# Cross attention's queries: seven block products per pair of heads in place of two plain projections, in a two-layer decoder trunk

## The chip, the cores and the metric

The kernel runs on one core of one Trainium2 chip. The metric is the device time of one launch in microseconds (us), the median of the runs. The engines are named as in the profile: PE (TensorE, matmuls), PEld (its weight loads), DVE (VectorE), ACT (ScalarE), POOL (GpSimd), SP (SyncE, which issues most loads). Each engine works through its own queue in order.

## The reference

A trunk of two layers over 512 tokens of width 1024, with 256 memory tokens. Each layer is a half-step SwiGLU FFN, a token mixer (layer 0: differential attention; layer 1: a pooling mixer), cross attention into the memory with 4 heads of 256, and a second FFN; each is followed by a LayerNorm of a scaled residual sum. The part that the change touches:

```python
def memory_cross_attention(x, mem, wq, wkv, wo):
    q = (x @ wq).reshape(B, S, XA_HEADS, XA_HEAD_DIM)          # wq 1024x1024
    k, v = jnp.split(mem @ wkv, 2, axis=-1)                    # wkv 1024x2048
    ...
    s = jnp.einsum('bshd,bmhd->bhsm', q, k) * (XA_HEAD_DIM ** -0.5)
    p = jax.nn.softmax(s, axis=-1)
    o = jnp.einsum('bhsm,bmhd->bshd', p, v).reshape(B, S, D_MODEL)
    return o @ wo

x = layer_norm(a * x + h, ...)                                 # h: the mixer
x = layer_norm(a * x + memory_cross_attention(x, mem, ...), ...)
```

## The kernel before, in words

**Products.** Every product is in fp32 split into two parts: a "high" part `wh` or `xh`, rounded by a copy on ACT, and a "low" part `wl` or `xl`, the difference, by a subtraction on DVE (`split`, lines 114 and 115; `split_scaled`, 119 and 120, for scaled queries). One product step is three matmuls, high by high, low input, low weight (`mm3`, lines 201, 202 and 203). A weight piece is 128x1024 of fp32, 512 KB: it is loaded into a raw tile, copied to a high and subtracted to a low tile.

**Cross attention** has, for each of four heads, keys and values of the memory (`xa_kv`: 48 matmuls of 256 columns to PSUM tile `pk`, 48 to `pv`), queries (`project` into `xq`: two 128-wide column blocks x 8 steps x 3 = 48 matmuls of 512 columns), and the scores, softmax and weighted values (`xa_head`, PSUM `xs`, `pt`, `xo`). `xa_main` is the main line; `xa_side` gives the heads' side work, and `weave` puts a side step between the products when 2500 ns of estimated matmul time have passed. `to_tokens` ends the stage with the output product (`ps`) and the next LayerNorm. Of the two layers' queries there are 8 heads x 48 = 384 matmuls of 512 columns.

**Into the stage.** The mixer's last products add to the residual `X` (`ln_add`, line 397); `ln_token` then does a token block's LayerNorm: the mean (L406, DVE), squares on ACT, the reciprocal deviation on POOL, and two passes on DVE (L423, L425). `turn` transposes a normalized block of 128 tokens on PE into PSUM tiles `pt` (L479), and splits them into `xh`, `xl`, the stage's input, feature rows on the partitions. With two 512-feature halves that is two ACT copies and two DVE subtractions of 128x512 per token block. The blocks are called tokens 0 to 3. While the last LayerNorms run, PE is given keys and values: in layer 0 head 0's, in layer 1 heads 0 and 1's (`early_kv`), woven into the pooling mixer.

**Loads.** In layer 0 weights for queries, keys and values come 1 MB at a time through 2 raw tiles (`raw_cols`) on SP's queue, with 5 high and 5 low tiles. In layer 1 512 KB pieces go through two tags, `raw` (2) and `rawe` (3), split into `wh`/`wl` or `we`. Layer 0 also writes the split memory (`mem`) to DRAM, 4 x 512 KB (`keep_memory`, SP's queue), for layer 1 to load again.

**Seven products.** The FFNs already compute their 2x2-block products with seven block products instead of eight. The x block sums for that are called factors; `turn` stores a token's transposes as `self.factors` when the next stage is an FFN. The order of instructions on each engine comes from the program's order and a scheduler's priorities; `issue_after` puts an instruction behind another.

Of the kernel before, what the change touches and what calls it, by code (L numbers as in the profile page):

```python
# [96 lines left out]
WAIT = object()  # L97


def drain(units):  # L100
    for _ in units:
        pass


class Trunk:
# [57 lines left out]
    def stage_pools(self, w, raw, order):  # L163

        with ExitStack() as ctx:
# [8 lines left out]
            self.w_bufs, self.raw_bufs, self.aux_turn = w, raw, 0  # L174
            self.w_order, self.raw_order = [("wh", "wl")], ["raw"]
# [9 lines left out]
    def aux(self, name, tag=None):  # L185
        if tag is None:
            tag = list(self.banks)[self.aux_turn % 3]
            self.aux_turn += 1
# [66 lines left out]
    def load(self, shape, src, tag=None):  # L255
# [4 lines left out]
        self.nc.sync.dma_start(t, src)  # L260
        return t

    def load_cols(self, w, c0, tag=None):
        if "rawe" not in self.stage:
# [5 lines left out]
    def load_wide(self, w, c0, tag=None):  # L270
        if "rawe" not in self.stage:
# [50 lines left out]
    def rows(self, w, k0, kn, c0, homes=None):  # L322
# [3 lines left out]
        for k in range(0, kn, 4):  # L326
# [5 lines left out]
            if "rawe" in self.stage:  # L332
# [122 lines left out]
    def turn(self, t, half, two_pass=None):  # L455
# [6 lines left out]
        if self.ln_next == "ffn":  # L462
# [687 lines left out]
    def pool_mixer(self, layer, ln):  # L1150
# [35 lines left out]
        self.w_order = [("wh", "wl")] * 3 + [("we", "we")] * 2  # L1186
        self.raw_order = ["rawe"] * 3 + ["raw"] * 2
        self.begin_ln(layer, ln, 1.0)
        for t in range(NT):
# [17 lines left out]
            self.turn_late()  # L1207
# [41 lines left out]
    def xa_kv(self, w, h, ahead=None):  # L1249
        nc = self.nc  # L1250
        rk = ahead or self.load_cols(w, h * 256)
        ps = self.mm("pk").rearrange("p (c n) -> p c n", c=2)
        for j in range(2):
            wk = rk[j] if ahead else self.halves(rk[j])
            for k in range(KC):
# [3 lines left out]
        kv = lambda: tuple(  # L1259
            self.kvp.tile([P, 2, MEM], F32R, tag="kv", name="kv", bufs=8) for _ in range(2)  # L1260
        )
        kt = kv()
        self.turn_late()
        self.split(kt[0], kt[1], ps)
        wv = self.halves_wide(self.load_wide(w, D + h * 256))
        ps = self.mm("pv").rearrange("p (m n) -> p m n", m=2)
        for m in range(2):
            o = slice(m * P, (m + 1) * P)
            for k in range(KC):
                mt = self.memT[k]  # L1270
                yield self.mm3(ps[:, m], (mt[0][:, o], mt[1][:, o]), wv[k], k == 0, k == KC - 1)
        v = kv()
        self.split(v[0], v[1], ps)
        return kt, v

    def xa_head(self, qs, kt, v):
# [3 lines left out]
        for tt in range(0, NT, 2):  # L1280
            sc = self.aux("xs").rearrange("p (t n) -> p t n", t=2)
            for i in range(2):
                o = slice((tt + i) * P, (tt + i + 1) * P)
                for c in range(2):
                    q = qs[c]
                    self.mm3(
                        sc[:, i], (q[0][:, o], q[1][:, o]), (kt[0][:, c], kt[1][:, c]), c == 0, c == 1
                    )
# [12 lines left out]
        for tt in range(0, NT, 2):  # L1301
# [8 lines left out]
            yield  # L1310
# [209 lines left out]
```

## Time and profile before

| | us |
|---|---|
| median of 3 runs | 1952.09 |
| runs | 1949.88, 1952.63, 1952.09 |
| the profiled execution's own time | 1952.38 |
| its span | 1950.6 |
| PE busy | 1918.7 (98%) |
| DVE busy | 1560.5 (80%) |
| ACT busy | 1012.7 (52%) |
| POOL busy | 336.1 (17%) |

The span is from the first to the last instruction on record; the run's time is 1.8 us more. Cross attention of layer 0 starts at about 601 us of the span, with the first `pk` matmul, and that of layer 1 at about 1455. A row of a timeline gives the start, the duration, the engine, the line, what is written and read, the shape, and in square brackets an idle time before it with what released it. A matmul's duration overlaps its neighbours', so that its cost is the distance of two starts. A row `x2` has two instructions.

### The profile page before, as it was taken

The page shows a single profiled execution, that of the slowest core. Times are in us where ns is not written, and L with a number is a line of the kernel's source. Part 1 is how long each engine was busy: PE and PEld are TensorE (multiplying, and loading weights), DVE is VectorE, ACT ScalarE, POOL GpSimd, SP SyncE. Part 2 cuts the span into 40 slices and gives each one's busy share as a digit, 9 for nine tenths or more (in the row PEclk, how much of TensorE's full clock was granted, in tenths as well). Part 3 has the DMA queues.
Part 4 walks back from the last instruction along what each step waited for, and adds up shares of the span by engine and source line. Part 5 has one row for each costly group of instructions (what it writes and reads, how often), then busy time and mean ns, then how long its engine had stood idle before and what let it go on. Part 6 is the DMA issues. An engine that isn't in the chain of part 4 may idle for free.

```text
span 1950.6 us, 32439 instructions
## 1 busy us (share of the span) xinstructions
PE 1918.7 (98%) x13052; PEld 1746.2 (90%) x13052; DVE 1560.5 (80%) x2200; ACT 1012.7 (52%) x1537; POOL 336.1 (17%) x317
## 2 busy tenths in 40 slices
PE   9999999999999999999999999999999999999998
PEld 8999998888778888989998999999888889999996
DVE  7988987788867557798887888888876468888886
ACT  6555553466655444555554555455445436555552
POOL 3212121111211002312210322112110013111211
PEclk9999999999999999999999999999999999999999
DMA  9888772322135325977695598778435336778861
GB/s 253 197 174 180 167 152 66 90 65 87 44 108 177 126 65 141 218 171 147 149 200 143 105 210 173 174 162 163 153 119 162 109 87 116 189 172 172 182 143 44
DMA packets 254182, 280.58 MB, mean 144 GB/s; under 512 B 9168, under 2 KB 221648, under 8 KB 254032
## 3 DMA queue, kind: packets, MB, share of 16 engines
q0 software_dynamic: 95808, 102.77, 32.4%
q1 hardware_dynamic: 158224, 175.74, 28.3%
q8 instruction: 102, 1.67, 0.3%
q14 instruction: 48, 0.39, 0.1%
HBM read 274.28 MB, written 4.20 MB: 143 GB/s over the span
## 4 chain that ended last, share of the span: by engine, by line
PE 79%; DVE 13%; ACT 3%; issue 3%; DMA 2%; POOL 1%; SPq 0%; DVEq 0%; POOLq 0%; ACTq 0%
PE x L201 7%; PE x L202 7%; PE x L203 7%; PE z L201 4%; PE z L202 4%; PE z L203 4%; PE ps L203 4%; PE ps L202 4%; PE ps L201 4%; DVE wl L115 3%; PE px L201 2%; PE px L203 2%; PE px L202 2%; PE y L203 2%; PE xq L201 2%
## 5 line engine op out<-in xcount | busy, mean ns | idle before, releaser
L636 POOL DMA_DIRECT2D ra<-in_ffn_w_in_dram x132 | 170.5, 1315 | 993.3 <-DVE wl L115 971.3
L114 ACT CAST wh<-ra 128x1024 fp32r<-128x1024 f32 x184 | 193.3, 1052 | 213.8 <-PE x L202 67.7
L115 DVE TENSOR_TENSOR wl<-ra,wh 128x1024 fp32r<-128x1024 f32 x184 | 223.6, 1220 | 70.8 <-ACT wh L114 64.7
L114 ACT CAST wh<-rc 128x1024 fp32r<-128x1024 f32 x136 | 142.9, 1053 | 120.6 <-PE x L202 45.5
L201 PE MATMUL x<-xh,wh 128*128 128x256 f32 x704 | 197.1, 280 | 1.5 <-ACT xh L114 0.8
L203 PE MATMUL x<-xh,wl 128*128 128x256 f32 x704 | 196.6, 279 | 1.9 <-DVE wl L115 1.9
L202 PE MATMUL x<-xl,wh 128*128 128x256 f32 x704 | 196.3, 279 | 0.0
L201 PE MATMUL x<-xe,wh 128*128 128x256 f32 x704 | 195.7, 278 | 0.0
L202 PE MATMUL x<-xe,wh 128*128 128x256 f32 x704 | 195.6, 278 | 0.0
L203 PE MATMUL x<-xe,wl 128*128 128x256 f32 x704 | 195.5, 278 | 0.0
L114 ACT CAST wh<-b 128x1024 fp32r<-128x1024 f32 x112 | 117.8, 1051 | 131.8 <-PE x L202 63.5
L115 DVE TENSOR_TENSOR wl<-rc,wh 128x1024 fp32r<-128x1024 f32 x136 | 164.4, 1219 | 22.9 <-ACT wh L114 22.9
L115 DVE TENSOR_TENSOR wl<-b,wh 128x1024 fp32r<-128x1024 f32 x112 | 136.7, 1221 | 41.6 <-ACT wh L114 41.6
L201 PEld LDWEIGHTS x<-xh,wh 128*128 128x128 f32 x704 | 133.0, 189 | 3.5 <-ACT xh L114 1.1
L203 PEld LDWEIGHTS x<-xh,wl 128*128 128x128 f32 x704 | 133.3, 189 | 2.4 <-DVE wl L115 2.4
L202 PEld LDWEIGHTS x<-xl,wh 128*128 128x128 f32 x704 | 133.4, 189 | 1.5 <-DVE xl L115 0.2
L201 PEld LDWEIGHTS x<-xe,wh 128*128 128x128 f32 x704 | 132.6, 188 | 1.4
L202 PEld LDWEIGHTS x<-xe,wh 128*128 128x128 f32 x704 | 132.5, 188 | 1.3
L203 PEld LDWEIGHTS x<-xe,wl 128*128 128x128 f32 x704 | 132.5, 188 | 0.0
L203 PE MATMUL y<-xh,wl 128*128 128x256 f32 x352 | 99.1, 281 | 2.1 <-DVE wl L115 1.2
L201 PE MATMUL y<-xh,wh 128*128 128x256 f32 x352 | 98.2, 279 | 0.1
L201 PE MATMUL z<-xe,wh 128*128 128x256 f32 x352 | 97.9, 278 | 0.0
(404 smaller groups left out, 6085.8 us busy)
## 6 DMA issues: line engine op xcount, KB each, us to landing
ra<-in_ffn_w_in_dram POOLq DMA_DIRECT2D x132, 512.0 KB, 6.9
rc<-in_ffn_w_in_dram SPq DMA_DIRECT2D x88, 512.0 KB, 6.2
b<-in_ffn_w_out_dram SPq DMA_DIRECT2D x60, 512.0 KB, 4.9
ra<-in_ffn_w_in_dram SPq DMA_DIRECT2D x44, 512.0 KB, 4.7
rc<-in_ffn_w_in_dram POOLq DMA_DIRECT2D x44, 512.0 KB, 7.5
b<-in_ffn_w_out_dram POOLq DMA_DIRECT2D x16, 512.0 KB, 13.0
raw<-in_da_w_qkv_dram SPq DMA_DIRECT2D x16, 512.0 KB, 5.1
raw<-in_xa_wkv_dram SPq DMA_DIRECT2D x8, 1024.0 KB, 5.4
```

The costliest lines, as they stand in the source:

```text
L114: self.nc.scalar.copy(hi, src),
L115: self.nc.vector.tensor_sub(lo, src, hi.bitcast(F32)),
L201: mm(out, w[0], x[0], start=start, stop=False, skip_group_check=again)
L202: mm(out, w[0], x[1], start=False, stop=False, skip_group_check=again)
L203: self.last_mm = mm(out, w[1], x[0], start=False, stop=stop, skip_group_check=again)
L636: self.last_more = nc.gpsimd.dma_start(t, source(*block), accum_op=ALU.add)
```

## The change

- **Queries.** `queries` handles a pair of heads (512 columns of `wq`) as a 2x2 block product: block rows are 512 features, block columns one head, input blocks 512 features by 256 tokens. Seven products of 24 matmuls with 256 columns replace 2 x 48 with 512, so a layer has 336 narrow for 192 wide ones. They run in the order factor 0 (weight r1), 1 (r2), 3 (r3), 6 (r4), 4, 5, 2.
- **Weight sums.** The third weight, r3, gets a second 512 KB added in its raw tile by an accumulating transfer on POOL's queue ahead of the first product; the other three sums are additions of 128x1024 on DVE (line 1408 after), in the raw tiles. So each of r1 to r4 stays in a raw tile from its load to its last use.
- **Input sums.** `x_factors` makes the factors for tokens 2 and 3 as they are transposed: two sums of 128x1024 of tokens 0 and 1, then per token an ACT copy, four sums and five splits. Tokens 0 and 1 are stored plainly.
- **Combining.** The products are combined by copies on ACT and additions of 128x512 on DVE, and four scaled splits per pair.
- **Order.** Keys and values yield in steps (`MARK`), interleaved with products. In layer 1 only head 0's keys and values are woven into the mixer, head 1's with the first pair's products. The weave's gap is 2200 instead of 2500.
- **Loads and tiles.** In layer 0 now 512 KB pieces through 5 raw tiles, with 4 high and 4 low tiles; in layer 1 2 high and 2 low tiles (3 and 3 before) beside 4 `we`.
- **Memory.** `keep_memory` is put behind the stage's last weight load on SP's queue (its four writes stand after the first four loads of the output weights).

The instructions: PE 13,095 rows against 12,809, DVE 1,990 against 1,900, ACT 1,157 against 1,103, POOL 190 against 185, SP 229 against 220.

```diff
@@ Trunk.turn
-        if self.ln_next == "ffn":
+        if self.ln_next in ("ffn", "xa"):
             hi, lo = self.factors[half]
@@ pool_mixer
-        self.w_order = [("wh", "wl")] * 3 + [("we", "we")] * 2
+        self.w_order = [("wh", "wl")] * 2 + [("we", "we")] * 2
...
-            self.turn_late()
+            if self.late and self.late[0] < 2:
+                self.turn_late()
             self.ln_token(t)
@@ x_factors (new)
+        temps = [self.tmp("q", (P, 4, H)) for _ in range(6)]
+        s3, a11, a12, a21, s1, s2 = temps
+        def part(i, x, o):
+            self.split(F[i][0][:, :, o], F[i][1][:, :, o], x)
+        for r, (hi, lo) in zip((a11, a12), F):
+            nc.vector.tensor_tensor(r, hi.bitcast(F32), lo.bitcast(F32), ALU.add)
+        yield
+        for t in (2, 3):
...
+            nc.scalar.copy(b21, pts[0])
+            nc.vector.tensor_tensor(t1, pts[1], b21, ALU.subtract)
+            part(3, t1, o)
+            part(2, pts[1], o)
+            nc.vector.scalar_tensor_tensor(t2, t1, -1.0, a11[:, :, o], ALU.mult, ALU.subtract)
+            nc.vector.scalar_tensor_tensor(t1, t2, -1.0, a12[:, :, o], ALU.mult, ALU.subtract)
+            part(6, t1, o)
+            yield
+            part(4, t2, o)
+            nc.vector.tensor_tensor(t3, a11[:, :, o], b21, ALU.subtract)
+            part(5, t3, o)
+            yield
@@ queries (new)
+        r1 = self.load([4, H], source(1, 1), tags[0])
+        r2 = self.load([4, H], source(2, 1), tags[1])
+        r3 = self.load([4, H], source(1, 2), tags[2])
+        nc.gpsimd.dma_start(r3, source(1, 1), accum_op=ALU.add)
+        yield MARK
+        x = bank(self.mm("xq"))
+        yield from product(x, r1, 0, True)
...
+        yield from product(y, r2, 1, True)
+        nc.vector.tensor_tensor(p1, y, p1, ALU.add)
+        qa = self.pair("q", (P, 2, S))
+        keep(qa, first, p1, 1)
+        yield MARK
+        r4 = self.load([4, H], source(2, 2), tags[3])
+        z = bank(self.aux("z", "yz"))
+        yield from product(z, r3, 3, True)
...
+        yield from product(z, r4, 6, then=(r4, r3))
+        yield MARK
+        yield from product(x, r4, 4, then=(r1, r4, ALU.subtract))
...
+        yield from product(x, r1, 5, then=(r2, r4))
...
+        yield from product(x, r2, 2)
@@ xa_main
-            for p in ((0, 2 * P), (2 * P, S)) if self.late else ((0, S),):
-                for c in range(2):
-                    yield from self.project(ps[c], ws[c], (p,))
-                    self.turn_late(1 - c)
...
+        ready = self.x_factors()
+        if not layer:
+            k = self.xa_kv(wkv, 0)
+            next(k)
+            yield from step(k)
+            self.turn_late(2)
+            yield from step(k)
+        self.late = []
+        next(ready)
+        if not layer:
+            for _ in range(2):
+                yield from step(k)
+                next(ready)
+        for u in range(XA_H // 2):
+            q = self.queries(wq, u, tags)
+            next(q)
+            k = self.xa_kv(wkv, u + 1, bank="yz")
+            next(k)
+            order = (k, q, k, q, k, q, k, q, q, q, q) if layer and not u else (q, k) * 4 + (q,) * 3
+            for g in order:
+                yield from step(g)
+                next(ready, None)
+        yield from whole(self.xa_kv(wkv, XA_H - 1))
@@ xa
-        self.weave(self.xa_main(layer), self.xa_side(), 2500)
+        self.weave(self.xa_main(layer), self.xa_side(), 2200)
...
-            self.keep_memory()
+            with self.tc.issue_after(self.last_load.ins):
+                self.keep_memory()
@@ pools
+    def xa_pools(self):
+        order = ("wh", "wl", "raw")
+        return self.stage_pools(dict(wh=4, wl=4), dict(raw=5), order, True)
...
-        return self.stage_pools(dict(wh=3, wl=3, we=4), dict(raw=2, rawe=3), order)
+        return self.stage_pools(dict(wh=2, wl=2, we=4), dict(raw=2, rawe=3), order, True)
@@ cross mixer of layer 1
-                    self.weave(self.early_kv(layer, (0,), ahead), side, 900, 6000)
-                drain(self.early_kv(layer, (1,)))
+                self.weave(whole(self.xa_kv(w, 0, ahead)), side, 900, 6000)
```

DVE's queue in layer 0, before, from the end of token 3's LayerNorm on (`X3`; `pt` are transposed tokens, `pk` keys, `raw` a raw weight):

```order
L425 SCALAR_TENSOR_TENSOR X3_79<-X3_79,rstd_6677,v_6459 128x1024
L115 TENSOR_TENSOR xl_6467<-pt_6851,xh_6465 128x4x128
L115 TENSOR_TENSOR xl_6468<-pt_6858,xh_6466 128x4x128
L115 TENSOR_TENSOR kv_6850<-pk_6792,kv_6849 128x512
L115 TENSOR_TENSOR xl_6467<-pt_6865,xh_6465 128x4x128
L115 TENSOR_TENSOR xl_6468<-pt_6872,xh_6466 128x4x128
L115 TENSOR_TENSOR wl_6947<-raw_6944,wh_6946 128x1024
L115 TENSOR_TENSOR wl_6951<-raw_6944,wh_6950 128x1024
```

The same place after the change (`q` are temporaries of the input sums):

```order
L441 SCALAR_TENSOR_TENSOR X3_79<-X3_79,rstd_6677,v_6459 128x1024
L130 TENSOR_TENSOR kt_6860<-pk_6800,kt_6859 128x512
L1370 TENSOR_TENSOR q_6864<-xh_6465,xl_6467 128x1024
L1370 TENSOR_TENSOR q_6865<-xh_6465,xl_6467 128x1024
L1384 TENSOR_TENSOR q_6867<-pt_6907,q_6866 128x4x128
```

Behind the LayerNorm the two wide sums now come first. Further on in the same queue, DVE after the change up to the split of head 1's second key weight (`xe` are factors 4 to 6, `y` and `p` the second product and its sum):

```order
L1392 TENSOR_TENSOR q_6863<-q_6864,q_6866 128x4x128
L130 TENSOR_TENSOR xe_6795<-q_6867,xe_6792 128x4x128
L1440 TENSOR_TENSOR p_6999<-y_7055,p_6999 128x512
L130 TENSOR_TENSOR xe_6794<-q_6863,xe_6791 128x4x128
L130 TENSOR_TENSOR wl_7090<-raw_6968,wh_7089 128x1024
```

Five rows stood before the first weight split; now 26 stand between the LayerNorm and `wl_7090`, five of them 128x1024.

DVE's queue in layer 1 after, from the second sum of tokens 0 and 1 to the split of factor 3 for token 3, the third product's input:

```order
L1370 TENSOR_TENSOR q_16296<-xh_16084,xl_16086 128x1024
L1384 TENSOR_TENSOR q_16298<-pt_16347,q_16297 128x4x128
L130 TENSOR_TENSOR kt_16429<-pk_16313,kt_16428 128x512
L1387 SCALAR_TENSOR_TENSOR q_16299<-q_16298,q_16295 128x4x128
L1392 TENSOR_TENSOR q_16294<-q_16295,q_16297 128x4x128
L130 TENSOR_TENSOR xl_16087<-q_16298,xh_16085 128x4x128
L130 TENSOR_TENSOR xl_16087<-pt_16347,xh_16085 128x4x128
L1388 SCALAR_TENSOR_TENSOR q_16298<-q_16299,q_16296 128x4x128
L1384 TENSOR_TENSOR q_16298<-pt_16437,q_16297 128x4x128
L1440 TENSOR_TENSOR p_16391<-y_16452,p_16391 128x512
L130 TENSOR_TENSOR xe_16293<-q_16298,xe_16290 128x4x128
L130 TENSOR_TENSOR xl_16087<-q_16298,xh_16085 128x4x128
```

Before, the tokens' plain splits stood here, one behind the other, between weight splits:

```order
L115 TENSOR_TENSOR wl_16211<-rawe_16206,wh_16210 128x1024
L115 TENSOR_TENSOR xl_15840<-pt_16107,xh_15838 128x4x128
L115 TENSOR_TENSOR xl_15841<-pt_16114,xh_15839 128x4x128
L115 TENSOR_TENSOR wl_16215<-rawe_16208,wh_16214 128x1024
L115 TENSOR_TENSOR kv_16185<-pv_16135,kv_16184 128x512
L115 TENSOR_TENSOR we_16282<-rawe_16276,we_16281 128x1024
```

Two rows of 128x512 per token block have become nine, and the weight splits stand behind them.

195 lines of the change are left out of this document (136 added, 59 removed).

## The prediction

> **What bounds the kernel now.** First the page's busy shares and its chain that ended last: they say whose time the span is.
>
> ```profile
> PE 1918.7 (98%) x13052; PEld 1746.2 (90%) x13052; DVE 1560.5 (80%) x2200; ACT 1012.7 (52%) x1537; POOL 336.1 (17%) x317
> PE 79%; DVE 13%; ACT 3%; issue 3%; DMA 2%; POOL 1%; SPq 0%; DVEq 0%; POOLq 0%; ACTq 0%
> ```
>
> TensorE (PE) is busy for 98% of the span, so fewer matmul columns are worth their time, wherever nothing else ends late. But VectorE (DVE) is 80% busy over the whole program and holds 13% of the chain: there is little slack to give it work. Then the busy times by window, in the two stretches of cross attention that the change rewrites (columns: window, then PE, PEld, DVE, ACT, POOL busy with their counts, the granted clock, the DMA share, GB/s).
>
> ```profile
> 615.20:745.00 129.80, 129.80 (x775) 113.89 (x775) 69.76 (x112) 52.63 (x101) 0.00 (x0) 1.00 0.34 109
> 1456.80:1460.20 3.40, 3.15 (x15) 3.15 (x16) 2.95 (x6) 2.55 (x5) 0.18 (x1) 0.50 0.03 9
> 1480.00:1500.00 20.00, 20.00 (x146) 18.84 (x146) 9.56 (x15) 10.04 (x17) 0.00 (x0) 1.00 0.60 172
> ```
>
> In layer 0 PE has no gap from 615.2 to 745.0 while DVE is busy for 69.8 of 129.8 us. In layer 1 the stretch from 1480 is full too, but ahead of it there is one of 3.4 us at half clock. PE's timeline shows what brought that: two idles of over a microsecond within 2 us.
>
> ```profile
> 1455.51 0.38 PE L201 MATMUL pk<-mem,wh 128*128 128x256 f32 x1 [1.24 <-ACT wh L241]
> 1457.05 1.12 PE L479 MATMUL pt<-ident,X 128*128 128x128 f32 x4 [1.04 <-DVE X L425]
> ```
>
> So in these stages a wait of PE is paid once as idle and can be paid again in clock: 3.4 us at half speed is 1.7 us of work.
>
> **The sum is made against the profiled execution**, 1952.38 us, 0.29 above the median of 1952.09.
>
> **Queries: 384 matmuls of 512 columns become 672 of 256.** Steady rows of each shape on PE's timeline of layer 1:
>
> ```profile
> 1474.45 0.39 PE L201 MATMUL xq<-xh,wh 128*128 128x512 f32 x1
> 1479.81 0.39 PE L203 MATMUL xq<-xh,wl 128*128 128x512 f32 x1
> ```
>
> These are 23 matmuls apart: 5.36 / 23 = 0.233 us each. The narrow shape stands in the keys of layer 0:
>
> ```profile
> 605.07 0.28 PE L202 MATMUL pk<-mem,wh 128*128 128x256 f32 x1
> 607.57 0.28 PE L203 MATMUL pk<-mem,wl 128*128 128x256 f32 x1
> 608.68 0.28 PE L203 MATMUL pv<-wh,mem 128*128 128x256 f32 x1
> 609.15 0.28 PE L201 MATMUL pv<-wh,mem 128*128 128x256 f32 x1
> ```
>
> The keys' two rows are 22 apart, 0.1136 each; the values' are 4 apart, 0.1175. I take 0.1155. Each layer loses 192 x 0.233 = 44.7 and gains 336 x 0.1155 = 38.8, which is -5.9; both layers **-11.8** (-13.1 at 0.1136, -10.4 at 0.1175). The Trainium skill, page "TensorE: Matmul & The Clock Gate", section "Back-to-back issue gap", gives a lone matmul's gap as N/2.4 + 2.5 ns, that is 215.8 and 109.2 ns, by which the saving would be only 9.5 us and the sum below +3.6. The rows above are longer for both widths, and they decide.
>
> **Layer 0: DVE gets a queue that PE catches up with.** The plain stores of tokens 2 and 3 were two DVE rows each; now two sums of 128x1024 come first, then nine rows of 128x512 per token. Rows of DVE that give the prices (a row's start to the next one's):
>
> ```profile
> 604.64 1.22 DVE L115 TENSOR_TENSOR wl<-raw,wh 128x1024 fp32r<-128x1024 f32 x1
> 605.77 1.28 DVE L423 SCALAR_TENSOR_TENSOR X<-X,mean,v 128x1024 f32<-128x1024 f32 x1
> 608.11 1.28 DVE L425 SCALAR_TENSOR_TENSOR X<-X,rstd,v 128x1024 f32<-128x1024 f32 x1
> 609.30 1.28 DVE L115 TENSOR_TENSOR xl<-pt,xh 128x512 fp32r<-128x512 f32 x2
> 610.50 0.68 DVE L115 TENSOR_TENSOR kv<-pk,kv 128x512 fp32r<-128x512 f32 x1
> 611.10 1.27 DVE L115 TENSOR_TENSOR xl<-pt,xh 128x512 fp32r<-128x512 f32 x2
> ```
>
> A 128x1024 row takes 1.13, one of 128x512 0.60. From 609.3, when the last token's LayerNorm leaves DVE, the new queue up to the low half of head 1's second key weight (the row wl_7090) holds 6 wide and 21 narrow rows: 6 x 1.13 + 21 x 0.60 = 19.4, so it is there at 628.7. PE, from the transposes at 607.68, has ahead of the first matmul that reads it 126 matmuls of 256 (14.6) and 16 transposes (1.6): it is there at 623.8. PE then idles **4.9 us**, if DVE never waits. But its rows follow ACT's copies, and one weight (head 1's first value piece) can only be issued when the fifth raw tile is free; with the waits that I find by walking both queues it is up to 7.0. I take 6.0. Behind the waiting matmul the whole of PE's queue stands, the third product among it. Two idles that add up to 2.3 us brought the half clock above, so +1.7 (0 to 1.7). Nothing later gives this back: from 615.2 to 745.0 PE had no idle that could shrink.
>
> **Layer 1: the same at the third product.** Rows of DVE there:
>
> ```profile
> 1463.22 0.68 DVE L397 SCALAR_TENSOR_TENSOR X<-X,ps 128x512 f32<-128x512 f32 x1
> 1463.82 1.22 DVE L243 TENSOR_TENSOR we<-rawe,we 128x1024 fp32r<-128x1024 f32 x1
> 1468.72 1.41 DVE L423 SCALAR_TENSOR_TENSOR X<-X,mean,pooled 128x512 f32<-128x512 f32 x2
> 1470.04 1.41 DVE L425 SCALAR_TENSOR_TENSOR X<-X,rstd,pooled 128x512 f32<-128x512 f32 x2
> 1471.37 0.68 DVE L115 TENSOR_TENSOR kv<-pk,kv 128x512 fp32r<-128x512 f32 x1
> ```
>
> From 1463.22, until the third product's input of token 3 is split, the new queue holds a LayerNorm sum (0.60), three weight splits (3.4), the mean (0.1), two passes of LayerNorm (1.32 each), the two wide sums (2.3) and 11 narrow rows (6.6): 15.6, so 1478.9, and up to 1480.7 where it waits for POOL and ACT. PE has in that time, after the transposes of token 2 (its row is below), 46 matmuls of 256 and token 3's transposes, then 49 matmuls to the third product.
>
> ```profile
> 1463.59 1.03 PE L479 MATMUL pt<-ident,X 128*128 128x128 f32 x8
> ```
>
> That is 1463.6 + 0.8 + 5.3 + 0.8 + 5.7 = 1476.2, an idle of 2.7 to 4.5; I take **3.6**, and +1.7 of clock (0 to 1.7). Against it stand before's own idles on this stretch, of which some go: -0.9 (-0.5 to -1.3, from the 1.24 and 1.04 above and this one):
>
> ```profile
> 1465.10 0.39 PE L203 MATMUL pk<-mem,we 128*128 128x256 f32 x1 [0.47 <-DVE we L243]
> ```
>
> **Weight sums and combinations.** A pair adds three 128x1024 sums, three adds of 128x512 and four scaled splits in place of the two per head: 3 x 1.13 + 3 x 0.60 = 5.2 us of DVE and about 1 us of ACT copies per pair, 10 us a layer. After the first third product PE's 130 us cover it (DVE is busy 70 of them), and PE is in front nowhere else by my walk but at the second pair's start: **+1.0** (0 to 2) for the two layers. If the cover were gone, 20 us of DVE would be on the path. The early sum is an accumulating transfer on POOL's queue, ahead of product 3 by two products (5.5 us) and the keys between. The nearest rows:
>
> ```profile
> ra<-in_ffn_w_in_dram POOLq DMA_DIRECT2D x132, 512.0 KB, 6.9
> raw<-in_da_w_qkv_dram SPq DMA_DIRECT2D x16, 512.0 KB, 5.1
> ```
>
> A plain 512 KB on POOL's queue lands in 6.9; even twice that is earlier than the split of r3 stands in DVE's queue (629 in layer 0, if issued by 612), so 0; a gain is excluded since before had no such wait. **The memory's write** (four transfers of 512 KB on SP's queue) moves from about 600 us behind the output weights' first four loads: both places are under a full PE, and in the second nothing that PE needs within 10 us is issued behind it: 0 on either side.
>
> The sum: -11.8 + 6.0 + 1.7 + 3.6 + 1.7 - 0.9 + 1.0 = **+1.3**, so 1953.7 for such an execution and, 0.3 lower, about **1953.5** for the median. All terms at their low ends: -13.1 + 4.9 + 0 + 2.7 + 0 - 1.3 + 0 = -6.8; at the high ends: -10.4 + 7.0 + 1.7 + 4.5 + 1.7 - 0.5 + 2.0 = +6.0.
>
> **Rivals.**
>
> *Faster: the queues keep pace and the clock holds.* DVE never waits for ACT, and the idles leave the clock alone: -11.8 + 4.9 + 2.7 - 1.3 = -5.5, or 1946.6 for the median. For it stands a stretch of layer 0's mixer with 1.34 us of PE idle and the clock at 1.00:
>
> ```profile
> 498.00:504.00 6.00, 4.66 (x28) 3.80 (x28) 5.22 (x13) 3.74 (x10) 1.16 (x1) 1.00 0.04 15
> ```
>
> Against it: the two idles here would be nearly three and over four times as long. Chance 0.25.
>
> *About the same, with one fall of the clock fewer.* The one idle of 3.6 us in layer 1 may leave the clock as that single one did, where it fell after two with work between them: 1.7 less, 1951.8. By the Trainium skill, page "TensorE: Matmul & The Clock Gate", Part 1, the clock goes down after an idle window of about 3.4 us; the fall at 1456.8, after idles of 1.24 and 1.04, doesn't agree with so long a window. Chance 0.12.
>
> *Slower: the raw tiles are the bound.* In layer 0 r1 to r3 hold three of the five raw tiles, and head 1's two key pieces, its two value pieces and r4 pass through the other two, each issued only when a split before it is done. r4 is issued when the row wl_7090 is done (628.7 or later) and, by the 5.1 above, lands at 634; copy and split make it 636, and PE reaches it at about 636.5. That has half a microsecond to spare. If such a load takes the 6.9 of POOL's queue, or the cast stands behind another copy, each of the four pairs waits 1 to 1.5 us more: +4 to +6 on the sum, about 1958.5. It decides from 5.6 us of landing upward. For it: the stretch from 1480 already moves 172 GB/s. Against it: the 5.1 is a median under load. Chance 0.27.
>
> That the change doesn't do what it says is excluded by the order of instructions, which has 672 matmuls of 256 columns on the queries.
>
> **How the numbers follow.** The forecast has the other 0.36. A measurement of this kernel tells 0.2% apart, 3.9 us: below 1948.2 is faster, above 1956.0 slower. Faster is the first rival, 0.25; the same is the forecast and the fewer fall of the clock, 0.48; slower is the raw tiles', 0.27. The range is 1946.6 to 1959: from the first rival to just past the high ends of all terms (1958.1 for the median), with the most of the third rival.
>
> **What would show it.** PE idle of 5 to 7 us before a pk matmul with wl near 624, released by DVE's split, and one of 3 to 4.5 before z near 1476, released by DVE's xl; a clock of 0.5 behind each; DVE without a gap from 609 to 628 and from 1463 to 1479; xq, y and z with 672 matmuls of 256, 0.116 apart. The prediction is wrong if these idles are under 2 us, if r4 or a raw load ends PE's waits, or if PE idles later in the stage, where I have 1.0 in all.

## The result and the profile after

The changed kernel takes 1973.07 us (median of 4 executions, 1966.86 to 1981.44) where the kernel before takes 1950.99 beside it. The ratio on record is 1.0118, with a 95% interval of 1.0077 to 1.0159 (the two medians alone give 1.0113). It is slower by far more than the range of the prediction allowed. The profiled execution of it took 1966.86, the fastest of the four, with a span of 1964.5. Its page's busy shares and chain:

```profile
PE 1913.9 (97%) x13340; PEld 1755.6 (89%) x13340; DVE 1615.4 (82%) x2268; ACT 1039.2 (53%) x1577; POOL 337.0 (17%) x321
PE 72%; DVE 16%; ACT 4%; DMA 3%; issue 3%; POOL 1%; DVEq 0%; POOLq 0%; ACTq 0%; SPq 0%
```

TensorE is busy for 4.8 us less than before, and the span is 13.9 longer: the time is in waits. PE has lost 7 points of the chain, and DVE, ACT and DMA have gained 5 (the shares are rounded). Where, the lengths of five stretches tell, each from one row of PE's timeline to another (first `pk` of layer 0, first `x` of the FFN behind it, last `ps` of the FFN ahead of the pooling mixer, first transposed token behind that mixer, first `x` of the last FFN, last matmul):

| stretch, us | before | after | difference |
|---|---|---|---|
| cross attention, layer 0 | 163.6 | 169.4 | +5.8 |
| the two FFNs between | 655.9 | 654.6 | -1.3 |
| pooling mixer up to its first transpose | 29.3 | 35.0 | +5.7 |
| cross attention, layer 1 | 164.2 | 169.0 | +4.8 |
| the last FFN | 327.6 | 326.3 | -1.3 |

Busy times in the three stretches that grew, of the kernel before (window; length, then PE, PEld, DVE, ACT, POOL, clock, DMA share, GB/s):

```profile
601.50:765.13 163.63, 162.72 (x979) 142.67 (x978) 99.33 (x155) 69.36 (x126) 10.62 (x10) 1.00 0.47 141
1420.99:1450.31 29.32, 27.46 (x231) 26.94 (x229) 21.60 (x34) 13.78 (x21) 4.37 (x4) 1.00 0.47 144
1450.31:1614.48 164.17, 161.00 (x932) 141.05 (x933) 104.80 (x174) 72.99 (x131) 13.39 (x15) 0.99 0.39 109
```

And of the changed kernel:

```profile
601.70:771.08 169.38, 161.67 (x1124) 148.84 (x1122) 126.51 (x189) 82.38 (x146) 11.82 (x12) 0.99 0.49 140
1425.66:1460.68 35.02, 29.08 (x230) 28.33 (x228) 26.76 (x40) 16.24 (x26) 6.19 (x6) 0.95 0.35 106
1460.68:1629.64 168.96, 158.62 (x1076) 145.48 (x1077) 129.74 (x205) 84.29 (x149) 12.03 (x16) 0.98 0.39 110
```

In both cross attentions DVE has 25 to 27 us more to do, and PE is no longer full. The middle row is the surprise: the mixer computes what it did before, and PE stands idle for 5.9 us of it, where it was 1.9 before, at a mean clock of 0.95.

**Layer 0.** PE's waits in the changed kernel:

```profile
615.81 0.39 PE L219 MATMUL xq<-xh,wl 128*128 128x256 f32 x1 [1.21 <-DVE wl L130]
620.55 0.38 PE L219 MATMUL pk<-mem,wl 128*128 128x256 f32 x1 [0.61 <-DVE wl L130]
630.15 0.35 PE L217 MATMUL pv<-wh,mem 128*128 128x256 f32 x1 [3.68 <-DVE p L1440]
630.72 0.39 PE L217 MATMUL xs<-kt,q 128*128 128x256 f32 x1 [0.22 <-ACT q L134]
631.79 0.58 PE L219 MATMUL pk<-mem,wl 128*128 128x256 f32 x1 [0.57 <-DVE wl L130]
```

They are 6.3 us up to the row that the prediction named; two more, 0.28 and 0.81, follow at 650 and 653. The last three rows belong together: in VectorE's queue the sum of the second product (L1440), whose PSUM bank the values need, stands two rows ahead of the second key weight.

```profile
613.93 0.69 DVE L1384 TENSOR_TENSOR q<-pt,q 128x512 f32<-128x512 f32 x1 [1.48 <-ACT q L1383]
627.51 0.69 DVE L130 TENSOR_TENSOR xe<-q,xe 128x512 fp32r<-128x512 f32 x1 [1.07 <-ACT xe L129]
629.32 0.68 DVE L1440 TENSOR_TENSOR p<-y,p 128x512 f32<-128x512 f32 x1
630.52 1.22 DVE L130 TENSOR_TENSOR wl<-raw,wh 128x1024 fp32r<-128x1024 f32 x1
```

Both waits of VectorE here are for ACT, and in ACT's queue the row waited for stands behind a weight's cast that had itself waited for a load from `wkv`: 2.74 us at 611.42 and 1.33 at 625.91. So the loads have a share in VectorE's delay.

**The pooling mixer.** On DVE's timeline one row ahead of it stands out, in the changed kernel:

```profile
1409.59 1.29 DVE L1152 TENSOR_TENSOR rawe<-rawe 128x512 f32<-128x512 f32 x2 [6.33 <-DMA rawe<-in_pool_w_dram]
```

Behind this row in DVE's queue stand the LayerNorms of the tokens that the mixer pools. Before, the same row waited like this:

```profile
1401.51 1.29 DVE L1136 TENSOR_TENSOR rawe<-rawe 128x512 f32<-128x512 f32 x2 [2.38 <-DMA rawe<-in_pool_w_dram]
```

The pooling weights come late because of what else is in flight. The reload of the memory from DRAM on GpSimd's queue, before:

```profile
1368.99 1.13 POOL L1247 DMA_DIRECT2D mem<-kept  x2 [13.06 <-DVE wl L115]
1391.23 1.06 POOL L1247 DMA_DIRECT2D mem<-kept  x2 [21.11 <-DVE wl L115]
```

And after the change:

```profile
1400.13 2.19 POOL L1264 DMA_DIRECT2D mem<-kept  x4 [40.46 <-DMA rawe<-in_xa_wkv_dram]
```

The pooling weights' line among the DMA issues of the changed kernel (the last number is us from issue to landing):

```profile
rawe<-in_pool_w_dram SPq DMA_DIRECT2D x2, 512.0 KB, 8.9
```

And in the kernel before:

```profile
rawe<-in_pool_w_dram SPq DMA_DIRECT2D x2, 512.0 KB, 4.4
```

Four transfers go out together at 1400 instead of two at 1369 and two at 1391, just as the pooling weights are issued, and these take 8.9 us instead of 4.4. The cause is a place in SBUF, as two experiments below show: the change lists layer 1's pools in another order, `we` ahead of `mem`, so the memory's tiles lie where something else still stands until 1400. PE then waits for the last token's LayerNorm:

```profile
1432.95 0.38 PE L218 MATMUL pv<-wl,mem 128*128 128x256 f32 x1 [1.12 <-DVE wl L130]
1439.24 0.33 PE L1192 MATMUL pp<-bandh,xh 128*128 128x128 f32 x1 [3.28 <-ACT xh L129]
1440.32 0.33 PE L1196 MATMUL pp<-bandh,xl 128*128 128x128 f32 x1 [0.76 <-DVE xl L130]
```

**Layer 1.** PE's longest waits:

```profile
1489.30 0.36 PE L217 MATMUL z<-xh,we 128*128 128x256 f32 x1 [2.14 <-ACT xh L129]
1490.41 0.38 PE L218 MATMUL z<-xl,we 128*128 128x256 f32 x1 [0.75 <-DVE xl L130]
1495.82 0.39 PE L218 MATMUL z<-xe,wh 128*128 128x256 f32 x1 [0.77 <-DVE xe L130]
1496.96 0.39 PE L218 MATMUL pv<-wl,mem 128*128 128x256 f32 x1 [0.75 <-DVE wl L130]
1503.61 0.39 PE L219 MATMUL xq<-xe,we 128*128 128x256 f32 x1 [0.94 <-DVE we L130]
1508.23 0.39 PE L217 MATMUL xq<-xe,we 128*128 128x256 f32 x1 [1.83 <-ACT p L1454]
1513.63 0.38 PE L217 MATMUL xq<-xh,wh 128*128 128x256 f32 x1 [0.56 <-DVE p L1460]
```

With a last one of 0.19 that is 7.9 us. (Three more, of 0.77, 1.22 and 1.06, stand at the start of the stage, where the kernel before has waits of 1.24 and 1.04 too.) The first six, 7.2 us, lie in a window in which DVE is busy for 27.7 of 28.6:

```profile
1480.30:1508.90 28.60, 21.42 (x171) 20.15 (x171) 27.71 (x36) 15.85 (x24) 1.33 (x1) 1.00 0.33 79
```

The two waits at the third product, 2.9 us, are the ones forecast. The others, 5.0 us, come as VectorE stays behind through product 6, head 1's values and products 4, 5 and 2.

**Time and clock.** Each execution has a mean granted clock. One minus it, times the span, is the most that half speed can have cost: idle time at half clock counts in it too, and so does the end of the program behind the last matmul, 2.5 us in the changed kernel's profile and 2.9 in that of before. In the four executions of the changed kernel:

| time, us | span | clock | lost to the clock | rest of the span |
|---|---|---|---|---|
| 1966.86 | 1964.5 | 0.994 | 11.8 | 1952.7 |
| 1971.33 | 1968.9 | 0.992 | 15.8 | 1953.1 |
| 1974.80 | 1972.4 | 0.990 | 19.7 | 1952.7 |
| 1981.44 | 1979.0 | 0.987 | 25.7 | 1953.3 |

The rest is the same to 0.6 us, and the spread of 14.6 goes with the clock (which is given to 0.001, or 2 us). The split isn't that good everywhere: with the memory's place undone (below) the rest is anything from 1949.4 to 1955.6 in four executions of one kernel. Over 66 executions of the kernel before, beside this study's kernels, the medians are 1951.55, 5.8 lost and a rest of 1944.1. So of the loss some 9 us are waits less what the products save, and 12 go with the clock. The medians of the kernel before beside the single experiments are 1951.21 to 1952.24, so that a difference of 1 us between two experiments says little. One execution of the kernel with factors 4 to 6 later took 2688.78 us at a mean clock of 0.653 and is left out of its figures below.

### The profile page after: what moved, and what is told of

The parts are those of the page before. It is cut to its first block, busy times and chain, and to the rows that moved or that the text cites. A ratio compares the mean times of both kernels' runs of the same rounds, so it can differ in the third digit from the quotient of the medians.

```text
span 1964.5 us, 33179 instructions
## 1 busy us (share of the span) xinstructions
PE 1913.9 (97%) x13340; PEld 1755.6 (89%) x13340; DVE 1615.4 (82%) x2268; ACT 1039.2 (53%) x1577; POOL 337.0 (17%) x321
## 4 chain that ended last, share of the span: by engine, by line
PE 72%; DVE 16%; ACT 4%; DMA 3%; issue 3%; POOL 1%; DVEq 0%; POOLq 0%; ACTq 0%; SPq 0%
PE x L218 6%; PE x L217 6%; PE x L219 6%; PE z L217 4%; PE z L219 4%; PE z L218 4%; DVE wl L130 4%; PE ps L219 3%; PE ps L218 3%; PE ps L217 3%; PE px L217 2%; PE px L219 2%; PE px L218 2%; PE y L219 2%; PE y L217 1%
## 5 line engine op out<-in xcount | busy, mean ns | idle before, releaser
L130 DVE TENSOR_TENSOR wl<-rc,wh 128x1024 fp32r<-128x1024 f32 x136 | 164.6, 1220 | 24.1 <-ACT wh L129 24.1
L219 PE MATMUL y<-xh,wl 128*128 128x256 f32 x376 | 105.6, 281 | 3.1 <-DVE wl L130 2.1
L218 PE MATMUL z<-xe,wh 128*128 128x256 f32 x376 | 104.5, 278 | 0.8 <-DVE xe L130 0.8
L217 PE MATMUL y<-xh,wh 128*128 128x256 f32 x376 | 105.0, 279 | 0.2 <-ACT wh L129 0.2
```

The source lines that it names most:

```text
L130: self.nc.vector.tensor_sub(lo, src, hi.bitcast(F32)),
L217: mm(out, w[0], x[0], start=start, stop=False, skip_group_check=again)
L218: mm(out, w[0], x[1], start=False, stop=False, skip_group_check=again)
L219: self.last_mm = mm(out, w[1], x[0], start=False, stop=stop, skip_group_check=again)
```

## The experiments

Theory A: VectorE's queue in both cross attentions, and the moved reload in the mixer, make TensorE wait, and the clock falls on top. The rivals are named with each.

**The memory's place undone.**

```diff
-        order = ("wl", "wh", "raw", "pT", "rawe", "we", "mem", "v", "kt")
+        order = ("wl", "wh", "raw", "pT", "rawe", "mem", "we", "v", "kt")
```

> The changed kernel with one thing undone: in layer 1 the memory tiles stand ahead of the we tiles in SBUF, as before the change, so that the reload of the memory from DRAM waits for what it waited for before. Theory A (the reload, four transfers at 1400 us in place of two at 1369 and two at 1391, collides with the pooling weights): the reload starts near 1373 and 1396 again, the pooling weights land in 4 to 5 us in place of 8.9, VectorE's wait of 6.3 us for them falls to about 2.4, TensorE's wait of 3.5 us in the pooling mixer falls under 1, and the kernel is 5 to 7 us faster than the changed one: about 1966 where that has 1973, ratio to before 1.007 to 1.009. Rival B (the mixer is late because it has fewer weight tiles and no keys of head 1): the reload moves but TensorE's wait in the mixer stays above 3 us, and the time stays at 1973.

Measured: 1963.41, ratio 1.0051 (1.0031 to 1.0071), 9.7 less than the changed kernel. On GpSimd's queue, and for DVE and PE, in this kernel:

```profile
1372.29 1.13 POOL L1264 DMA_DIRECT2D mem<-kept  x2 [13.21 <-DVE wl L130]
1395.18 1.07 POOL L1264 DMA_DIRECT2D mem<-kept  x2 [21.77 <-DVE wl L130]
...
1405.34 1.29 DVE L1152 TENSOR_TENSOR rawe<-rawe 128x512 f32<-128x512 f32 x2 [2.40 <-DMA rawe<-in_pool_w_dram]
...
1434.31 0.33 PE L1192 MATMUL pp<-bandh,xh 128*128 128x128 f32 x1 [0.40 <-ACT xh L129]
1435.40 0.33 PE L1196 MATMUL pp<-bandh,xl 128*128 128x128 f32 x1 [0.76 <-DVE xl L130]
```

The whole chain is as it was before the change, and rival B is out. The gain is larger than expected; by the clocks less is lost there too (8.9 at the median instead of 17.8), but with rests that vary by 6 us it stays open how the gain divides. The profiled execution is the longest of this kernel's four (1972.10; the others 1962.85 to 1963.57): in it the clock fell at 1436.2 and stayed at half for 23.9 us.

**The same place, given to the kernel before.**

```diff
-        order = ("wl", "wh", "raw", "rawe", "mem", "we")
+        order = ("wl", "wh", "raw", "rawe", "we", "mem")
```

> The kernel before with one thing taken from the change: in layer 1's pools the memory tiles stand behind the we tiles. All products are those of before. Theory A (the reload of the memory, moved to 1400 us, delays the pooling weights and so the LayerNorm behind them): the four transfers are issued near 1396 to 1400 together, VectorE waits for the pooling weights for 5 us or more in place of 2.4, TensorE waits 3 us or more in the pooling mixer, and the kernel takes 4 to 7 us more than before, with more time at half clock. Rival B (the place costs nothing by itself): within 2 us of before.

Measured: 1959.61, ratio 1.0035 (1.0021 to 1.0049), 7.4 more than before's 1952.24. This one edit, with all of before's products, brings back the whole chain:

```profile
1398.57 2.19 POOL L1247 DMA_DIRECT2D mem<-kept  x4 [39.63 <-DMA rawe<-in_xa_wkv_dram]
...
1408.35 1.29 DVE L1136 TENSOR_TENSOR rawe<-rawe 128x512 f32<-128x512 f32 x2 [6.39 <-DMA rawe<-in_pool_w_dram]
...
1437.48 0.48 PE L1176 MATMUL pp<-bandh,xh 128*128 128x128 f32 x1 [3.28 <-ACT xh L114]
```

The place alone is enough, and the queries' products have nothing to do with it. The pooling weights land in 8.4 us there.

**Factors 4 to 6 later.**

```diff
             part(2, pts[1], o)
+            yield
+        for t in (2, 3):
...
             nc.vector.scalar_tensor_tensor(t2, t1, -1.0, a11[:, :, o], ALU.mult, ALU.subtract)
...
+            when = (0, 2, 4, 5, 6, 7) if layer else (3, 4, 5, 6)
+            for i, g in enumerate(order):
...
+                if i in when:
+                    next(ready, None)
```

> The changed kernel with the input sums in another order: for tokens 2 and 3 first what factors 2 and 3 need, and the sums and splits of factors 4 to 6 only behind the weight splits of the second keys. The same instructions in all. Theory A (VectorE's queue is what TensorE waits for): in layer 0 the idle of 3.7 us before the values of head 1 goes, since the row that it waited for stands 14 rows earlier, and of the 6.3 us of idle between 615 and 632 at most 2 are left, with the half clock behind it; in layer 1 the 9.8 us between 1487 and 1514 fall by 2 to 5, as the queue there is full for longer. In all 7 to 11 us faster than the changed kernel, about 1964. Rival C (the wait is for the PSUM bank of the second product or for loads): the idles stay within 1 us of what they are, and the time at 1973.

Measured: 1962.25 (median of nine executions), ratio 1.0053 (1.0037 to 1.0069), 10.8 less. In layer 0 one wait is left between 604 and 632 (0.94, 0.80 and 0.20 follow behind it), and the FFN's first `x` is 162.3 behind the first `pk`, 1.4 less than in the kernel before:

```profile
620.43 0.38 PE L219 MATMUL pk<-mem,wl 128*128 128x256 f32 x1 [0.48 <-DVE wl L130]
```

The same instructions in another order on VectorE gave back 7.1 us of this stretch (169.4 to 162.3), and 2.4 in layer 1 (169.0 to 166.6). In layer 1 the waits from the third product on are 5.3 us, where the rows above make 7.9 (the expectation's 9.8 is too much). Theory A holds and rival C falls.

**Both edits**, the two diffs of the memory's place and of the later factors together.

> Both edits together: memory tiles ahead of the we tiles, and factors 4 to 6 behind the weight splits. Theory A: the two gains are in different stretches and add up, 12 to 17 us faster than the changed kernel: 1956 to 1961, still not faster than before by more than the seven products' saving less what is left of layer 1's idles. Rival: they do not add, because what one gives the other's wait takes, and it ends within 3 us of the better of the two.

Measured: 1956.76, ratio 1.0031 (1.0013 to 1.005). They add for the most part: 9.7 and 10.8 by themselves, 16.3 together.

**The values in another PSUM bank.**

```diff
-            k = self.xa_kv(wkv, u + 1, bank="yz")
+            k = self.xa_kv(wkv, u + 1, bank="px")
```

> The changed kernel with the values' PSUM tile of a pair in another bank (px) than the second and third product's (yz). Theory A (VectorE's queue): the idle of 3.7 us before the values goes, but the next matmul that reads the second key weight, two rows further on the same queue, waits in its place: in all 4 to 5 us of idle between 623 and 632, as in the changed kernel. Rival C (the bank is the cause): the idle goes and nothing takes its place, 4 us less in this stretch.

One execution, 1966.80. The wait moved to the next matmul, the sum of the three waits fell from 4.5 to 3.9, and the stretch is as long as it was (169.5, and 169.4 in the changed kernel):

```profile
630.04 0.39 PE L217 MATMUL xs<-kt,q 128*128 128x256 f32 x1 [3.32 <-ACT q L134]
631.12 0.58 PE L219 MATMUL pk<-mem,wl 128*128 128x256 f32 x1 [0.57 <-DVE wl L130]
```

The bank was only the first of several things behind one queue.

**The memory written early.**

```diff
-            with self.tc.issue_after(self.last_load.ins):
-                self.keep_memory()
+            self.keep_memory()
```

> The changed kernel with the memory's write to DRAM not put behind the stage's last load. My step was that its place costs nothing either way: within the spread of the changed kernel, 1966 to 1981. Rival: the write near 600 us delays the loads of head 0 and 1 and of r1 to r4, and TensorE waits for a raw tile there, 2 us or more slower in the stretch from 601 to 765.

Measured: 1976.00 (1971.23 to 1978.56), within the changed kernel's spread, and the stretch of layer 0 is 169.4 in both. The write's place costs nothing.

**The changed kernel again.**

> The changed kernel once more, unchanged, for more executions of it and a second profile. If the spread of its time is time at half clock, then the span less half of the time at half clock is again 1952.5 to 1954 in every execution, whether it takes 1966 or 1981; if the waits themselves differ from run to run, that figure varies by as much as the time does.

Measured: 1973.31 (1968.97 to 1978.14), ratio 1.0107 (1.0087 to 1.0128). The rest of the span is 1948.8 to 1950.5, 3 us below the first four, so that the number expected failed, and with it the claim of one rest for all executions; but within these four it varies by 1.7 while the time varies by 9.2. In this profile (1976.02) the pooling mixer's stretch is 45.1 us long where the first had 35.0. The row for what the clock's record shows as one fall:

```profile
1438.30:1465.60 27.30, 25.51 (x118) 25.32 (x119) 12.59 (x18) 8.30 (x13) 0.00 (x0) 0.50 0.33 97
```

PE has work for 25.5 of 27.3 us, all at half speed: matmuls of 256 columns start 0.213 us apart in it, and 0.117 apart otherwise. It is 23.9 us longer than the first profile's fall there, up to 12 us of work, which covers the whole difference of 9.2 between the two executions.

**More cover ahead of the pooling products**, on top of both edits.

```diff
-                self.weave(whole(self.xa_kv(w, 0, ahead)), side, 900, 6000)
+                self.weave(whole(self.xa_kv(w, 0, ahead)), side, 900, 8000)
```

> The kernel with both earlier edits (memory tiles back, factors 4 to 6 late), and 18 matmuls of head 0's values in layer 1 put ahead of the first pooling product, 2 us of cover, by a lead of 8000 ns in place of 6000. Theory D (what is left above before is time at half clock, and the long falls start at the wait of 1 us in the pooling mixer): the wait goes, no execution has more than 20 us at half clock, and the median falls from 1956.8 to 1952 to 1954. Rival E (the falls come from the waits in cross attention): the wait in the mixer goes, but 4 of 10 executions still have over 30 us at half clock, and the median stays within 2 us of 1956.8.

Measured: 1954.70 (1951.41 to 1956.78, 11 executions), ratio 1.0008 (0.9999 to 1.0016). The waits ahead of the pooling products (0.25 and 0.76 without this edit) are gone, and one of 0.70 stands later in the mixer. No execution lost more than 9.8 us to the clock, where without this edit 4 of 10 lost 15.7 to 17.7. That speaks against rival E and for theory D, though the median is 0.7 above its range. That the long falls come from this wait is likely, and not shown: the two kernels ran on different chips, and the one profile of the kernel without the edit has no long fall in it. The kernel before has the same waits (0.40 and 0.76); 3 of its 17 executions beside the last experiment lost 13.7 to 15.7, and none of the other 49 over 9.8. The time is now level with before's, not ahead of it. Layer 0's stretch is now 162.1, 1.5 shorter than before, and layer 1's 166.5, 2.3 longer.

**The weight sums on GpSimd**, on top of both edits.

```diff
-            nc.vector.tensor_tensor(t, x, t, op)
+            nc.gpsimd.tensor_tensor(t, x, t, op)
```

> The kernel with both earlier edits, and the twelve weight sums of 128x1024 on GpSimd in place of VectorE. Theory A (in layer 1 VectorE's queue is full from 1463 to 1500, and the sums are part of it): if GpSimd's sums take less than 3 us each and do not slow VectorE, the 7 us of idle that are left in layer 1 fall to 4 and the median by 2 to 4 us, to 1953 to 1955. Rival F (the sums are on the path wherever they run, and GpSimd is slower): TensorE waits for the sum itself before products 4 and 5 in each pair, 1 to 3 us longer each than now, and the kernel is 4 to 10 us slower than with the sums on VectorE.

Measured: 1975.17, ratio 1.0117 (1.0103 to 1.0131), 18.4 more. Rival F, and more than that. The longest waits of PE are 7.07 us in layer 0 and 4.78 in layer 1; then GpSimd's rows in layer 1, and VectorE's in the same microseconds:

```profile
639.91 0.58 PE L217 MATMUL z<-xe,wh 128*128 128x256 f32 x1 [7.07 <-ACT xe L129]
...
1495.22 2.88 POOL L1415 TENSOR_TENSOR rawe<-rawe 128x1024 f32<-128x1024 f32 x1
1498.18 5.45 POOL L1415 TENSOR_TENSOR raw<-rawe,raw 128x1024 f32<-128x1024 f32 x2
...
1495.09 3.57 DVE L130 TENSOR_TENSOR xe<-q,xe 128x512 fp32r<-128x512 f32 x1
1501.34 0.68 DVE L1327 TENSOR_REDUCE mx<-xs 128x2 f32<-128x512 f32 x1
1501.94 2.77 DVE L130 TENSOR_TENSOR we<-rawe,we 128x1024 fp32r<-128x1024 f32 x1
```

A sum takes 2.6 to 2.9 us by the means of its groups, and VectorE rows with both inputs in SBUF that meet one take about as long (2.77 to 3.57; such a row of 128x512 takes 0.69 alone, one of 128x1024 1.22), so that nothing is taken off VectorE. The row that reads PSUM takes its usual 0.68. The Trainium skill, page "SBUF — State Buffer", section "SBUF: two separate sides", describes this: the two engines share a port pair, and whichever starts first holds it for its whole instruction. The rows agree in that each of VectorE's ends only behind GpSimd's, 0.6 to 1.1 us later; by its recorded start the first of them was 0.13 us ahead of GpSimd's and still the one that waited.

**Two of three sums by transfers**, on top of the three edits.

```diff
         yield from product(x, r1, 0, True)
+        nc.sync.dma_start(r1, source(2, 2))
+        nc.gpsimd.dma_start(r1, source(1, 2), accum_op=ALU.add)
...
-        yield from product(x, r4, 4, then=(r1, r4, ALU.subtract))
+        nc.gpsimd.dma_start(r2, r4, accum_op=ALU.add)
+        yield from product(x, r4, 4)
...
-        yield from product(x, r1, 5, then=(r2, r4))
+        yield from product(x, r1, 5)
```

> The kernel with the three earlier edits (memory tiles back, factors 4 to 6 late, more cover ahead of the pooling products; 1954.7), and two of a pair's three weight sums taken off VectorE: the first weight is loaded anew and added to by an accumulating transfer, the second gets the fourth added by one. VectorE loses 8 rows of 128x1024, 9 us, half of them in layer 1. Theory A (VectorE's full queue is what is left in layer 1): the idles between 1477 and 1506, 6 us now, fall by 2 to 4, and the median to 1951 to 1953. Rival G (the new transfers land later than VectorE's sum would be done): TensorE waits before the sixth or seventh product of a pair, 1 us or more in place of what goes, and the median is 1955 to 1962.

Measured: 1964.64, ratio 1.006 (1.0048 to 1.0073). Rival G, and slower than its range: in layer 1 PE stands for 6.2 us ahead of product 5, the sixth in order. ACT's queue shows why:

```profile
1504.95 0.58 PE L217 MATMUL xq<-xe,we 128*128 128x256 f32 x1 [6.19 <-ACT p L1464]
...
1502.43 1.04 ACT L129 CAST wh<-raw 128x1024 fp32r<-128x1024 f32 x1 [6.40 <-DMA raw<-rawe]
1504.33 0.58 ACT L1464 COPY p<-xq 128x512 f32<-128x512 f32 x1
```

PE waits for ACT's copy of product 4's result, which frees the PSUM bank. The copy stands in ACT's queue behind the cast of the last product's weight, and that waits for the transfer which adds the fourth weight to the second (`raw<-rawe`, 8.0 us from issue to landing). So it was this transfer; the reloaded weight had been cast by 1495.5.

**The sums left out**, on top of the three edits: products 4, 5 and 2 use unsummed weights.

```diff
-            if then:
-                add(*then)
```

> The kernel with the three earlier edits, with the three sums of the weights on VectorE left out in every pair, so that products 4, 5 and 2 use unsummed weights. It bounds what the sums cost from below. My term for them and the combinations was 1.0 us in both layers. Theory A now: in layer 1 they are 3.4 us of a queue that is full, so at least 2 us of the 6 us of idle go there, and 3 to 4 us in all; the stretch from the first transposed token to the FFN falls from 166.5 to 163 to 164.5. Rival: under 1 us in all, as I had it.

Measured: 1953.18, 1.5 less than with them by the medians and nothing by the ratios (1.0007 and 1.0008, whose intervals overlap). The stretch of layer 1 is 165.2, 1.3 less; that of layer 0 is 163.6, 1.5 more. The theory's 3 to 4 us was too much: the three sums by themselves cost at most 1.5 us, and it isn't shown that they cost anything.

**Other work between the products**, on top of the three edits.

```diff
+                n = self.xa_kv(wkv, 2, bank="yz")
+                order = (k, q) * 4 + (q, n, n, q, q) if layer else (q, k) * 4 + (q, n, n, q, q)
...
+                order = (q, k) * 3 + (q,) * 4
```

> The kernel with the three earlier edits (1954.7), and in both layers the first 24 matmuls of head 2's keys put between the fifth and the sixth product of the first pair: more work of TensorE where VectorE's queue is full, none added. Theory A: of the idles before products 4, 5 and 2 in layer 1 (0.64, 0.75, 0.68, 1.35 and 0.88 in the kernel with three edits) those behind the inserted work go, 1.5 to 2.8 us, less one weight split of VectorE; the median is 1952 to 1953.5, level with before or up to 0.05% faster. Rival H (the fifth raw tile holds the key piece and the next pair's weights come later): an idle of 1 us or more at the start of the second pair takes the place, and the median stays at 1954 to 1956.

Measured: 1958.04, ratio 1.0027 (1.0012 to 1.0041). Rival H, larger than it was put: the waits behind the inserted work went, and the second pair of layer 1 starts late. PE waits for VectorE to free the bank; VectorE's row stands behind a weight's split, and that weight landed 8.9 us after its issue.

```profile
1507.89 0.58 PE L217 MATMUL xq<-xh,we 128*128 128x256 f32 x1 [5.00 <-DVE q L135]
...
1504.93 1.04 ACT L129 CAST wh<-raw 128x1024 fp32r<-128x1024 f32 x1 [5.42 <-DMA raw<-in_xa_wq_dram]
```

## Why the prediction was wrong, point by point

By stretches, in the first profile: the pooling mixer grew by 5.7 us where I had nothing, cross attention by 5.8 in layer 0 where my terms make +1.8, and by 4.8 in layer 1 where they make -1.5, with 1.0 more for both; the FFNs are 2.6 shorter.

- **The saving.** Right in size where nothing waits: the narrow matmuls run 0.117 apart in the changed kernel (the rows below are 7 apart), which makes 10.8 us where I had 11.8.

```profile
661.08 0.28 PE L217 MATMUL y<-xh,wh 128*128 128x256 f32 x1
661.90 0.28 PE L218 MATMUL y<-xl,wh 128*128 128x256 f32 x1
```

- **Layer 0's wait.** The mechanism is right, and the sum, 6.3 for 6.0 with 1.7 of clock for 1.7, in part by luck. The wait that I had forecast, up to the second key weight, is the last three rows, 4.5 us, less than my low end of 4.9; the other 1.8 are two waits for earlier weight splits that my walk didn't have. The key weight's row ended at 631.74; 2.6 of the 3.0 us beyond 628.7 are the two waits for ACT. The largest part fell one bank earlier than I had it, on the same queue. The stretch still grew by 4 us more than these terms make. By the starts of PE's rows, 1.5 of that is missing saving (without idle the query rows take 45.3 us before and 40.9 after, 4.4 less where I had 5.9), 0.8 is more idle in all, and by 1.7 the other rows take longer beyond what the clock took; why, no run shows.
- **Layer 1's wait.** The wait at the third product came as forecast, 2.9 us (2.7 to 4.5). Mis-sized is the term behind it, 1.0 for both layers: it measured 5.0 in layer 1, and 1.1 in layer 0. I walked VectorE's queue to the third product and took the rest as covered, "after the first third product PE's 130 us cover it". But a queue that is late at one product is late at the next until PE has more to do per product than VectorE, and VectorE stayed full until 1508.9. An average over 130 us hid 28 us in which it had no slack.
- **The term that failed: there was none for the pooling mixer.** "The memory's write ... 0 on either side" looked at where the memory is written, and that step was right. I did not follow where it is read back: the tiles' new place in SBUF holds back the reload, and that is 5.7 us of the first profile, and in whole executions 7.4 us by itself in the kernel before and 9.7 in the changed one.
- **The clock.** I priced a fall at 1.7 us. In the first profile it was that, five times up to the last matmul. In others one fall lasted 23.9 or 27.3 us, 12 to 14 us of work, and over the eight executions of the changed kernel the median lost is 18.7 where before has 5.8. That is over half of the result.
- **The rivals.** The slower one, raw tiles, didn't happen as put: no wait of PE in layer 0 names a load. Loads had a share by way of ACT's queue (2.74 and 1.33 us above). The two faster ones are out by the waits and falls that came. That nothing later gives time back holds: the FFNs are shorter by 1.3 each here, but over kernels with the same FFNs the longer stretch is anything from 654.1 to 657.1.
- **The three edits** show what the idea is worth. With the queue in order and the reload back, seven products gain 1.5 us in layer 0 and lose 2.3 in layer 1, where the token LayerNorms, the input sums and the weight sums all meet on VectorE in 30 us. These are single profiles, and layer 0's stretch is 163.6 and 164.6 in two kernels with the same code there (before, and before with the other place), so that 1 us isn't certain.

What stays open: what starts a long fall and what ends it. The long ones on record stand in the mixer at the pooling products' waits, and the cover, which took these waits away, took the long falls with them in 11 executions; that is no proof. Why the clock then stays at half for 4 to 8 times 3.4 us, with PE working, no run shows.

## What to carry to other kernels

Walk the queue of the engine that takes over the work until it has caught up, not until the first thing that waits for it. When a change touches a list of pools, look up what each transfer into them now waits for: a tile's place decides when a load far away may start. And count each idle of a full TensorE with what the clock may add, which can be ten times the idle: 0.40 and 0.76 us were followed by 23.9 us at half clock, some 12 us of work.

## What the runs showed of the hardware

- The granted clock can stay at half for 13.7, 23.9 or 27.3 us after waits of some 4 us, and once, for 23.9, after 0.40 and 0.76; each length is a multiple of 3.41. Matmuls of 256 columns start 0.213 us apart in it instead of 0.117. The same program loses 11.8 us to it in one execution and 25.7 in another.
- Four transfers of 512 KB beside two others make these land in 8.9 us instead of 4.4 (8.4 in the kernel before with the place alone changed).
- A 128x1024 sum takes 2.6 to 2.9 us on GpSimd and 1.22 on VectorE, and VectorE's rows with both inputs in SBUF take up to five times as long beside it (3.57 for 0.69).
